# A hybrid attention step: the reciprocal ahead of a shared tile's transposes, its second half parted a block later, and a one-operand select on GpSimd

## The chip, the cores and the metric

The kernel runs on one core of a Trainium2 chip. The metric is the time of one execution on the device in microseconds; the figure for the kernel before is the median of three runs. The engines are named as the profile names them: PE is TensorE, with PEld its weight loads; DVE is VectorE, ACT is ScalarE, POOL is GpSimd, SP is SyncE, which issues DMAs.

## The reference

One layer with two parallel mixers over 1024 latent tokens and 128 context tokens, width 1024, head size 64, 8 query heads and 2 key heads in each mixer. Mixer A attends to all keys. Mixer B attends to a band of 128 tokens on either side and to the context, with a learned sink logit in the softmax. The part that the change touches is mixer B:

```python
valid = (jnp.abs(rel)[None] <= WINDOW) & (abs_j >= 0) & (abs_j < n)
s_band = jnp.where(valid[None, :, None, None], s_band, NEG_INF)
...
s = jnp.concatenate([sink_column(sink, kv, s_ctx.shape[:-1]), s_ctx, s_band], axis=-1)
p = jax.nn.softmax(s, axis=-1).astype(v_lat.dtype)
p_ctx = p[..., 1:1 + n_ctx]
p_band = p[..., 1 + n_ctx:]
o = (jnp.einsum('bnkgqs,bskd->bnqkgd', p_ctx, v_ctx)
     + jnp.einsum('bnkgqs,bnskd->bnqkgd', p_band, vband))
```

Both outputs are multiplied with a SiLU gate, put side by side, multiplied with `w_out` and added to the residual.

## The kernel before

After the projections the attention runs over units `(t, m, g)`: token tile `t` of 128 queries, mixer `m` (0 is A, 1 is B), key head `g` with its four query heads. They stand in the order `(1,0,0), (1,1,0), (1,0,1), (1,1,1), (2,0,0)` and so on, so units with an odd number are of mixer B. A unit of mixer A has nine key blocks, one of mixer B four (three for the first and last tile), and each block is one step of the main loop. At a step `s` the loop runs what has been put off to it (`tick`, filled by `later`), makes the weights of the step's block (`scores`), runs what the list `due` holds for the step, issues some matmuls of the output projection, and multiplies the weights of the block of three steps ago with the values (`values`). Nothing is reordered afterwards: on each engine the instructions stand in the order in which the code issues them, and each engine works its own list in order.

Products are made of two parts, a rounded `ph` and the rest `pl`, so a block of weights is exponentiated on ScalarE (L1305), rounded there (L1309, or L1290 and L1298 in mixer B), and the rest is made on GpSimd (L1313, L1291) or VectorE (L1299). `values` multiplies both parts (L1323, L1326).

A unit of mixer B gets its weights ahead, while the unit of mixer A before it runs. `weight_items` makes the scores with queries on the partitions (L1057, L1058), VectorE adds the mask (L1061), and ScalarE exponentiates them into `pen` and sums the rows (L1047). `finish` puts off the rest: the sink's exponential (`sinks`, L1091), its addition to the sum on GpSimd (`total`, L1094), and two steps after the weights the merging of `pair`. `divide` takes the reciprocal of the sum on VectorE (L1097), at the first step of the unit. One step later `turned` transposes the reciprocals on TensorE (`pti`, L1110), `put` copies them (L1114) and sends them to memory, and later they come back in rows and scale the unit's gates (L1120, L1106).

In the twelve *paired* units (mixer B, `1 < t < 8`) the band's first and last block share one tile. The first block has weights only where key >= query, the last only where key <= query, and both have the diagonal. `pair` therefore copies the last block into the empty half of the first on VectorE (L1015) and keeps of the last block only the diagonal, by a product with the identity on GpSimd (L1016). One step before the unit starts, `unpair` transposes the shared tile, four heads in one bank of PSUM (`st_pair`, L1024), and parts it: one VectorE instruction writes the first block's weights (L1026), a second copies the last block's over the diagonal (L1027). Blocks 1 and 2 of the unit are transposed as they come (L1297).

The PSUM banks that matter: tag B has two, shared by `st` and `st_pair`; tag A has two, shared by `pmx` (score maxima of a later unit of mixer A, L985, reduced on VectorE by L986 and at last L994), `sn` and `pti`.

Of the kernel before, what the change touches and what calls it, by code (L numbers as in the profile page):

```python
# [9 lines left out]
F32 = mybir.dt.float32  # L10
F32R = mybir.dt.float32r
BF16 = mybir.dt.bfloat16
I16 = mybir.dt.int16
AF = mybir.ActivationFunctionType
ALU = mybir.AluOpType
# [4 lines left out]
P = 128  # L20
# [54 lines left out]
EX_AT = (2, 2, 5)  # L75
ROWS_AT = (1, 1, 4, 6)
# [41 lines left out]
def hybrid_step(ctx, tc, x_prompt, x_sample, cache_k_a, cache_v_a, cache_k_b, cache_v_b,  # L118
# [3 lines left out]
    nc = tc.nc  # L122
# [13 lines left out]
    def later(n, f):  # L136

        agenda.setdefault(now[0] + n, []).append(f)
# [13 lines left out]
    def bank(tag, name):  # L152
        return ps.tile([P, 512], F32, tag=tag, name=name, bufs=BANKS[tag])
# [11 lines left out]
    ident_r = cst.tile([P, P], F32R, name="ident_r")  # L165
# [165 lines left out]
    with tc.tile_pool(name="st", bufs=2, side="right") as st:  # L331
# [4 lines left out]
                                channel_multiplier=1)  # L336
# [214 lines left out]
        for j in range(1, KT + 3):  # L551
# [68 lines left out]
            if KT - 2 <= j < KT:  # L620
# [3 lines left out]
                c0, n = W_QA.cols[0]  # L624
# [50 lines left out]
    with tc.tile_pool(name="qt", bufs=2, side="right") as qt:  # L675
# [29 lines left out]
        def query(pq, m, t, tabs, n=1):  # L705
# [19 lines left out]
            def rotated():  # L725

                qf = qt.tile([P, 4, 2, HD], F32, tag="qf", name=f"qf{nm}", bufs=3)
                out = qf.rearrange("p h g d -> p g h d")
                pair = lambda a: a.rearrange("p (g h) d -> p g h d", g=2)
                if t:  # L730
                    nc.vector.tensor_tensor(out, *(pair(a) for a in v["rot"]), op=ALU.add)
                else:
                    nc.vector.tensor_tensor(
                        out, pair(v["qn"]), gain4[:, 2 * m, :].unsqueeze(1).unsqueeze(1).to_broadcast([P, 2, 4, HD]),
                        op=ALU.mult)
                v["qf"] = qf
# [24 lines left out]
        for m in range(2):  # L761
            w, nxt = ((W_QA, W_QB), (W_QB, W_KV))[m]
            ts = list(range(1, NT)) + [0]
            for t in ts:
# [3 lines left out]
                if (m, t) in ((0, ts[-2]), (1, ts[GATE_AT[0]])):  # L768
                    n = len(wg) // 2
# [88 lines left out]
    def window(t):  # L858

        return (0 if t == 1 else POS[t - 2]), (12 if t == NL else POS[t] + 1)  # L860
# [6 lines left out]
    with ktp:  # L867
# [62 lines left out]
        for n, t in enumerate(KV_ORDER):  # L930
            if n < AHEAD:
                tick()
                pk, v = pks[n]
# [21 lines left out]
    qtile, qbtile, mxtile, sgl = {}, {}, {}, {}  # L955
    penat = {}
# [11 lines left out]
    def max_items(i):  # L968
# [37 lines left out]
                out.append(lambda h=h, b=b: item(h, b))  # L1006
        return out, finish

    def paired(t):

        return 1 < t < NL

    def pair(i):
        prev, nxt = (penat[i][:, :, o : o + P] for o in (0, 3 * P))
        nc.vector.copy_predicated(prev, mask[:, 0:P].bitcast(I16).unsqueeze(1).to_broadcast([P, 4, P]), nxt)  # L1015
        nc.gpsimd.tensor_tensor(nxt, nxt, ident_r.bitcast(F32).unsqueeze(1).to_broadcast([P, 4, P]), op=ALU.mult)  # L1016

    def unpair(i):

        prev, nxt = (penat[i][:, :, o : o + P] for o in (0, 3 * P))  # L1020
        over = mask[:, 3 * P : 4 * P].unsqueeze(1).to_broadcast([P, 4, P])
        s = bank("B", f"st{i}_pair")
        for h in range(4):
            nc.tensor.transpose(s[:, P * h : P * h + P], prev[:, h], ident_r.bitcast(F32))  # L1024
        s4 = s.rearrange("p (h n) -> p h n", h=4)
        nc.vector.scalar_tensor_tensor(prev, over, 0.0, s4, op0=ALU.is_ge, op1=ALU.mult)  # L1026
        nc.vector.copy_predicated(nxt, mask[:, 3 * P : 4 * P].bitcast(I16).unsqueeze(1).to_broadcast([P, 4, P]), s4)  # L1027

    def weight_items(i):

        t, m, g = units[i]
        v = {}

        def small(name):
            return qs.tile([P, 4], F32, tag=name, name=f"{name}{i}")

        def first(n):
            if t:
                penat[i] = qp2[0].tile([P, 4, 512], F32, tag="pen", name=f"pen{i}")[:, :, 0:n]
            else:  # L1040
                penat[i] = w3.tile([P, 512], F32, tag="pe", name=f"pen{i}", bufs=PES).rearrange(
                    "p (h n) -> p h n", h=4)
            for x in ("nm", "sum", "ex", "inv"):
                v[x] = small(x)

        def exp(h, s, scale):
            nc.scalar.activation(penat[i][:, h], s, AF.Exp, bias=v["nm"][:, h : h + 1], scale=scale,  # L1047
                                 accum_out=v["sum"][:, h : h + 1])

        def item(h):  # L1050
            p0, p1_ = window(t)
            n = P * (p1_ - p0)
            if h == 0:
                first(n)
            lhs = qtile[i][:, P * h : P * h + P]
            s = bank("DEEE"[h] if i == 3 else "A", f"sn{i}_{h}")[:, 0:n]
            nc.tensor.matmul(s, lhs, khb[:, g, p0:p1_, :], start=True, stop=False)  # L1057
            nc.tensor.matmul(s, lhs, klb[:, g, p0:p1_, :], start=False, stop=True)  # L1058
            m0 = P if t == 1 else 0

            nc.vector.tensor_tensor_reduce(s, s, mask[:, m0 : m0 + n], -1.0, nsink[:, 4 * g + h : 4 * g + h + 1],  # L1061
                                           op0=ALU.add, op1=ALU.min, accum_out=v["nm"][:, h : h + 1])
            later(1, lambda: exp(h, s, -1.0))

        def prompt():
            first(P)
            s = bank("A", f"sn{i}")
            for h in range(4):
                hs = slice(P * h, P * h + P)
                nc.tensor.matmul(s[:, hs], qtile[i][:, hs], khp[:, 2 + g, :], start=True, stop=False)  # L1070
                nc.tensor.matmul(s[:, hs], qtile[i][:, hs], klp[:, 2 + g, :], start=False, stop=True)
            mx = small("mx4")
            nc.vector.tensor_reduce(mx, s.rearrange("p (h n) -> p h n", h=4), axis=AX.X, op=ALU.max)
            nc.vector.scalar_tensor_tensor(v["nm"], mx, -1.0, nsink[:, 4 * g : 4 * g + 4], op0=ALU.mult, op1=ALU.min)
            for h in range(4):
                exp(h, s[:, P * h : P * h + P], 1.0)

        def finish():
            nc.gpsimd.tensor_tensor(v["ex"], v["nm"], sink[:, 4 * g : 4 * g + 4], op=ALU.add)
            if paired(t):  # L1080
                later(PAIR_AT, lambda: pair(i))
            if t:
                for n, f in zip(EX_AT if i > 3 else EX_EARLY, (sinks, total, divide)):
                    later(n, f)
            else:
                sinks()
                later(1, total)
                later(1, divide)

        def sinks():  # L1090
            nc.scalar.activation(v["ex"], v["ex"], AF.Exp)  # L1091

        def total():
            nc.gpsimd.tensor_tensor(v["sum"], v["sum"], v["ex"], op=ALU.add)  # L1094

        def divide():
            nc.vector.reciprocal(v["inv"], v["sum"])  # L1097
            if t == 0:
                for h in range(4):
                    nc.vector.tensor_scalar(penat[i][:, h], penat[i][:, h], v["inv"][:, h : h + 1], None, op0=ALU.mult)  # L1100
                return

            later(ROWS_AT[0], turned)
            later(ROWS_AT[1], put)
            later(ROWS_AT[2], rows)
            later(ROWS_AT[3], lambda: nc.gpsimd.tensor_tensor(sgl[i], sgl[i], v["rows"], op=ALU.mult))  # L1106

        def turned():
            v["pt"] = bank("A", f"pti{i}")[0:4, 0:P]
            nc.tensor.transpose(v["pt"], v["inv"], ident_r.bitcast(F32))  # L1110

        def put():
            iv = spare[0:4, 512 : 512 + P]
            (nc.vector.tensor_copy if i < 2 else nc.scalar.copy)(iv, v["pt"])  # L1114
            nc.sync.dma_start(r_dram[i // 2], iv)

        def rows():
            v["rows"] = spare[:, 512:768].rearrange("p (c n) -> p c n", c=2)
            for s in range(2):
                nc.sync.dma_start(v["rows"][HD * s : HD * s + HD],  # L1120
                                  r_dram[i // 2].rearrange("(c s) n -> s c n", s=2)[s : s + 1].to_broadcast([HD, 2, P]))

        return ([lambda h=h: item(h) for h in range(4)] if t else [prompt]), finish
# [42 lines left out]
    mask = qp.tile([P, 512], BF16, name="mask", bufs=1)  # L1166
# [116 lines left out]
    def scores(i, b, blk):  # L1283
# [3 lines left out]
        if m == 1 and paired(t) and blk[0] in (0, 3):  # L1287
            p = penat[i][:, :, P * blk[0] : P * blk[0] + P]
            ph4, pl4 = (a.rearrange("p (h n) -> p h n", h=4) for a in (ph, pl))
            nc.scalar.copy(ph4, p)  # L1290
            nc.gpsimd.tensor_tensor(pl4, p, ph4, op=ALU.subtract)  # L1291
            return ph, pl
# [138 lines left out]
    slots, start = [], []  # L1431
# [8 lines left out]
    def put(s, f):  # L1440
        due.setdefault(s, []).append(f)
# [23 lines left out]
    for i, (t, m, g) in enumerate(units):  # L1465
        if m and paired(t):
            put(start[i] - 1, lambda i=i: unpair(i))

    for k, at in enumerate(HELD):
        put(at, lambda k=k: held_gates(k))  # L1470
# [92 lines left out]
```

## Time and profile before

| | before |
|---|---|
| median of 3 runs | 703.16 us (703.07 to 703.47) |
| the profiled execution | 703.9 us, its span 702.2 us |
| granted TensorE clock | 0.999 |
| COPY_PREDICATED L1015 (12 times) | 754 ns |
| SCALAR_TENSOR_TENSOR L1026 (12 times) | 677 ns |
| COPY_PREDICATED L1027 (12 times) | 732 ns |
| RECIPROCAL L1097 (18 times, 12 of them paired) | 160 ns |
| transposes of the shared tile L1024 | 48 of 272 ns |

The durations are medians. The span runs from the first instruction to the last; some 1.7 us of the execution lie around it. A row of the timeline gives the start, the time from the start to the end, the engine, the line, the operation, output and inputs, and how many such rows follow each other; in brackets stands the idle time ahead and what ended it. A matmul's row begins when it is issued and ends when its last result is modelled to be out, so rows of following matmuls overlap.

### The profile page before, as it was taken

Reading aid. Unit: us, or ns where it says so; the run is one execution under the profiler, and the core shown is the slowest. Engines: PE = TensorE matmul, PEld = TensorE weight load, DVE = VectorE, ACT = ScalarE, POOL = GpSimd, SP = SyncE. Lnnn points to the kernel's source line nnn. Section 1 sums busy time; section 2 is a strip of 40 time slices with the busy share of each in tenths; the row PEclk is TensorE's granted clock in tenths of the full one; section 3 lists DMA queues with packets and bytes.
Section 4 is the critical chain, followed back from the end, with each engine's and each line's share of the span. In section 5 each row is a group of like instructions: output and inputs, shape, how many; then the busy total and the mean of one; then the engine's idle time right before and its main releaser. Section 6 shows DMA issues by size and latency. Waiting matters only on the chain.

```text
span 702.2 us, 10666 instructions
## 1 busy us (share of the span) xinstructions
PE 688.8 (98%) x3493; PEld 554.3 (79%) x3493; DVE 470.7 (67%) x1025; ACT 408.5 (58%) x848; POOL 387.4 (55%) x392
## 2 busy tenths in 40 slices
PE   8999999999999999999999999999999999999997
PEld 4679988878788889987777777787777777877876
DVE  4775258968778845756867677676776676675563
ACT  5666312412423433198876887787778768877770
POOL 3556033232223421278787867777786778686751
PEclk9999999999999999999999999999999999999999
DMA  8961283358443116423122121212221221212323
GB/s 342 405 244 61 79 304 76 90 151 262 113 115 112 34 42 218 129 92 102 46 83 76 45 84 53 90 40 75 67 84 32 83 75 45 84 54 90 96 78 120
DMA packets 54231, 78.50 MB, mean 112 GB/s; under 512 B 6952, under 2 KB 25496, under 8 KB 54176
## 3 DMA queue, kind: packets, MB, share of 16 engines
q1 hardware_dynamic: 45936, 65.86, 28.3%
q10 hardware_dynamic: 8240, 11.96, 6.3%
q8 instruction: 27, 0.44, 0.3%
q14 instruction: 28, 0.23, 0.1%
HBM read 58.63 MB, written 19.18 MB: 111 GB/s over the span
## 4 chain that ended last, share of the span: by engine, by line
PE 88%; DVE 6%; POOL 2%; issue 1%; ACT 1%; DMA 1%; SPq 0%; POOLq 0%; ACTq 0%; DVEq 0%
PE po L1404 13%; PE pv L1326 6%; PE pv L1323 5%; PE pq L268 5%; PE pq L266 5%; PE pq L267 5%; PE st L1303 4%; PE st L1302 4%; PE pmx L985 4%; PE pv L1325 4%; PE pg L280 3%; PE pg L276 3%; PE pg L281 3%; PE pk L267 2%; PE pk L268 2%; PE pk L266 2%
## 5 line engine op out<-in xcount | busy, mean ns | idle before, releaser
L1313 POOL TENSOR_TENSOR pl<-pe,ph 128x512 fp32r<-128x512 f32 x130 | 167.3, 1296 | 62.3 <-ACT ph L1309 49.2
L986 DVE TENSOR_REDUCE mx<-pmx 128x1 f32<-128x384 f32 x192 | 100.6, 550 | 50.1 <-PE pmx L985 49.6
L1305 ACT ACTIVATE pe<-st 128x512 f32<-128x512 f32 x146 | 86.7, 594 | 23.8 <-PE st L1303 22.7
L1309 ACT CAST ph<-pe 128x512 fp32r<-128x512 f32 x146 | 90.6, 621 | 5.5
L1323 PE MATMUL pv<-ph,v_hi 128*128 128x512 f32 x208 | 83.4, 401 | 0.1
L1326 PE MATMUL pv<-pl,v_hi 128*128 128x512 f32 x208 | 82.2, 395 | 0.9 <-POOL pl L1313 0.7
L184 POOL TENSOR_TENSOR rs_q<-ms_q,mhalf 128x8 f32<-128x8 f32 x18 | 34.1, 1897 | 80.8 <-DVE ms_q L182 80.8
L1061 DVE CUSTOM_DVE_ANT_0 sn<-sn,mask,nsink 128x512 f32<-128x512 f32 (+1 forms) x64 | 46.3, 724 | 43.8 <-PE sn L1058 41.4
L1404 PE MATMUL po<-wo,ogh 128*128 128x512 f32 (+1 forms) x224 | 73.3, 388 | 0.0
L985 PE MATMUL pmx<-kha,qt 128*128 128x384 f32 x192 | 59.7, 357 | 0.2 <-DVE mx L986 0.2
L1325 PE MATMUL pv<-ph,v_lo 128*64 128x512 f32 x146 | 57.7, 395 | 0.0
L1303 PE MATMUL st<-qb,kla 68*128 68x512 f32 x144 | 57.3, 398 | 0.0
L1302 PE MATMUL st<-qt,kha 128*128 128x512 f32 x144 | 57.1, 397 | 0.0
L1326 PEld LDWEIGHTS pv<-pl,v_hi 128*128 128x128 f32 x208 | 39.0, 188 | 18.4 <-POOL pl L1313 1.2
L1047 ACT ACTIVATE pen<-sn,nm 128x512 f32<-128x512 f32 (+2 forms) x72 | 44.9, 625 | 6.6 <-DVE nm L1061 3.1
L1404 PEld LDWEIGHTS po<-wo,ogh 128*128 128x128 f32 x224 | 41.0, 188 | 6.4 <-ACT ogh L1366 0.3
L1323 PEld LDWEIGHTS pv<-ph,v_hi 128*128 128x128 f32 x208 | 39.2, 188 | 8.1 <-issue 0.6
L1291 POOL TENSOR_TENSOR pl<-pen,ph 128x512 fp32r<-128x512 f32 x24 | 30.8, 1285 | 26.0 <-PE pv L1323 26.0
L744 ACT CAST qo0q<-ptq 128x512 fp32r<-128x512 f32 x18 | 10.6, 586 | 57.3 <-PE ptq L741 53.1
L1404 PE MATMUL po<-wo,ogl 128*128 128x512 f32 (+1 forms) x112 | 43.6, 389 | 0.0
L985 PEld LDWEIGHTS pmx<-kha,qt 128*128 128x128 f32 x192 | 35.3, 190 | 9.4 <-DVE mx L986 1.2
L466 POOL TENSOR_TENSOR h<-hf,h 128x256 fp32r<-128x256 f32 (+2 forms) x32 | 27.3, 876 | 19.8 <-ACT h L460 10.0
(260 smaller groups left out, 1768.7 us busy)
## 6 DMA issues: line engine op xcount, KB each, us to landing
qt<-qd SPq DMA_DIRECT2D x36, 256.0 KB, 2.9
wm<-in_w_mod_ss_dram SPq DMA_DIRECT2D x7, 1024.0 KB, 11.6
qd<-qo0q ACTq DMA_DIRECT2D x36, 128.0 KB, 2.4
qd<-qo1q ACTq DMA_DIRECT2D x36, 128.0 KB, 2.4
sgl<-gd SPq DMA_DIRECT2D x35, 128.0 KB, 2.5
out_dram<-yt SPq DMA_DIRECT2D x17, 256.0 KB, 2.1
xn<-in_x_sample_dram SPq DMA_DIRECT2D x8, 512.0 KB, 7.0
wg<-in_w_mod_g_dram SPq DMA_DIRECT2D x4, 1024.0 KB, 8.6
```

Source lines behind the costliest of these rows:

```text
L266: nc.tensor.matmul(out, h_at(0, i, k, tok), w.hi[k], start=(k == 0), stop=False)
L985: nc.tensor.matmul(pm[:, 0:384], lhs, kha[:, g, 3 * b : 3 * b + 3, :], start=True, stop=True)
L986: nc.vector.tensor_reduce(mx[:, h, b : b + 1], pm[:, 0:384], axis=AX.X, op=ALU.max)
L1302: nc.tensor.matmul(s, kh, qtile[i], start=True, stop=False)
L1303: nc.tensor.matmul(s, kl, qbtile[i], start=False, stop=True)
L1305: nc.scalar.activation(pe, s, AF.Exp)
L1309: nc.scalar.copy(ph, pe)
L1313: nc.gpsimd.tensor_tensor(pl, pe, ph, op=ALU.subtract)
L1323: nc.tensor.matmul(pv, two, ph, start=(b == 0), stop=False)
L1325: nc.tensor.matmul(pv[0:64, :], vl, ph, start=False, stop=False)
L1326: nc.tensor.matmul(pv, two, pl, start=False, stop=last)
L1404: nc.tensor.matmul(po[n, q.start], a, wo_parts[KT * n + k][lo][:, q], start=(k == KS[0] and p == 0), stop=(k == KS[-1] and p == 2))
```

## The change

For the paired units `divide` is no longer put off to the unit's first step: it is kept in `divided` and called at the head of `unpair`, in the step before, ahead of the transposes of the shared tile. What follows `divide` is put off by one step more, so it keeps its step. The second half of the parting, the COPY_PREDICATED, becomes `unpair_rest` and runs one step later. On GpSimd the product with the identity becomes an `affine_select`, which reads only the tile and writes zero off the diagonal. `sinks` and `total` keep their steps, and units that are not paired are as before.

```diff
+    divided = {}
...
     def pair(i):
         prev, nxt = (penat[i][:, :, o : o + P] for o in (0, 3 * P))
         nc.vector.copy_predicated(prev, mask[:, 0:P].bitcast(I16).unsqueeze(1).to_broadcast([P, 4, P]), nxt)
-        nc.gpsimd.tensor_tensor(nxt, nxt, ident_r.bitcast(F32).unsqueeze(1).to_broadcast([P, 4, P]), op=ALU.mult)
+        nc.gpsimd.affine_select(out=nxt, in_=nxt, pattern=[[0, 4], [-1, P]], compare_op=ALU.is_equal, fill=0.0, base=0,
+                                channel_multiplier=1)
+
+    shared = {}
 
     def unpair(i):
 
-        prev, nxt = (penat[i][:, :, o : o + P] for o in (0, 3 * P))
+        divided.pop(i)()
+        prev = penat[i][:, :, 0:P]
         over = mask[:, 3 * P : 4 * P].unsqueeze(1).to_broadcast([P, 4, P])
         s = bank("B", f"st{i}_pair")
         for h in range(4):
             nc.tensor.transpose(s[:, P * h : P * h + P], prev[:, h], ident_r.bitcast(F32))
-        s4 = s.rearrange("p (h n) -> p h n", h=4)
-        nc.vector.scalar_tensor_tensor(prev, over, 0.0, s4, op0=ALU.is_ge, op1=ALU.mult)
-        nc.vector.copy_predicated(nxt, mask[:, 3 * P : 4 * P].bitcast(I16).unsqueeze(1).to_broadcast([P, 4, P]), s4)
+        shared[i] = s.rearrange("p (h n) -> p h n", h=4)
+        nc.vector.scalar_tensor_tensor(prev, over, 0.0, shared[i], op0=ALU.is_ge, op1=ALU.mult)
+
+    def unpair_rest(i):
+        over = mask[:, 3 * P : 4 * P].bitcast(I16).unsqueeze(1).to_broadcast([P, 4, P])
+        nc.vector.copy_predicated(penat[i][:, :, 3 * P : 4 * P], over, shared.pop(i))
...
-            if t:
+            if paired(t):
+                later(EX_AT[0], sinks)
+                later(EX_AT[1], total)
+                divided[i] = divide
+            elif t:
                 for n, f in zip(EX_AT if i > 3 else EX_EARLY, (sinks, total, divide)):
                     later(n, f)
...
-            later(ROWS_AT[0], turned)
-            later(ROWS_AT[1], put)
-            later(ROWS_AT[2], rows)
-            later(ROWS_AT[3], lambda: nc.gpsimd.tensor_tensor(sgl[i], sgl[i], v["rows"], op=ALU.mult))
+            o = int(paired(t))
+            later(ROWS_AT[0] + o, turned)
+            later(ROWS_AT[1] + o, put)
+            later(ROWS_AT[2] + o, rows)
+            later(ROWS_AT[3] + o, lambda: nc.gpsimd.tensor_tensor(sgl[i], sgl[i], v["rows"], op=ALU.mult))
...
         if m and paired(t):
             put(start[i] - 1, lambda i=i: unpair(i))
+            put(start[i], lambda i=i: unpair_rest(i))
```

How the instructions move is shown at unit 11 (token tile 3, second key head), whose neighbours of mixer A are units 10, 12 and 14. The number behind a tile's name is its unit; line numbers of the changed kernel differ by the lines added. First VectorE, where the unit's shared tile is parted; before:

```order
L986 TENSOR_REDUCE mx12_4674<-pmx12_3_1_4943 128x1
L986 TENSOR_REDUCE mx12_4674<-pmx12_3_2_4946 128x1
L1026 SCALAR_TENSOR_TENSOR pen11_4757<-mask_2970,st11_pair_4951 128x4x128
L1027 COPY_PREDICATED pen11_4757<-mask_2970,st11_pair_4951 128x4x128
L1097 RECIPROCAL inv11_4761<-sum11_4759 128x4
L986 TENSOR_REDUCE mx14_4967<-pmx14_0_0_4968 128x1
L994 TENSOR_REDUCE m_nat0_109<-mx12_4674 128x4
L986 TENSOR_REDUCE mx14_4967<-pmx14_0_1_4989 128x1
```

And the same place of VectorE in the changed kernel:

```order
L986 TENSOR_REDUCE mx12_4673<-pmx12_3_1_4943 128x1
L986 TENSOR_REDUCE mx12_4673<-pmx12_3_2_4946 128x1
L1110 RECIPROCAL inv11_4761<-sum11_4759 128x4
L1032 SCALAR_TENSOR_TENSOR pen11_4757<-mask_2970,st11_pair_4952 128x4x128
L986 TENSOR_REDUCE mx14_4966<-pmx14_0_0_4967 128x1
L1036 COPY_PREDICATED pen11_4757<-mask_2970,st11_pair_4952 128x4x128
L994 TENSOR_REDUCE m_nat0_109<-mx12_4673 128x4
L986 TENSOR_REDUCE mx14_4966<-pmx14_0_1_4989 128x1
```

The reciprocal has moved up past the two instructions that part the tile, and the COPY_PREDICATED down past one reduction; the rows around them are the same.

On GpSimd the rows around the select of unit 11 are these in the changed kernel (`sum11` is the reciprocal's input, `pl10` the rest of the weights of unit 10, whose product is running):

```order
L1327 TENSOR_TENSOR pl10_5_4865<-pe10_5_4869,ph10_5_4864 128x512
L1368 TENSOR_TENSOR spare_3486<-spare_3486,sgl9_4639 128x256
L1018 AFFINE_SELECT pen11_4757<-pen11_4757 128x4x128
L1107 TENSOR_TENSOR sum11_4759<-sum11_4759,ex11_4760 128x4
L1327 TENSOR_TENSOR pl10_6_4893<-pe10_6_4897,ph10_6_4892 128x512
L1327 TENSOR_TENSOR pl10_7_4907<-pe10_7_4911,ph10_7_4906 128x512
L1327 TENSOR_TENSOR pl10_8_4935<-pe10_8_4939,ph10_8_4934 128x512
```

Before, the third row was a TENSOR_TENSOR of `pen11` and `ident_r` (L1016); no row has moved.

On TensorE, which waits for both, these rows stand around the transpose of the reciprocals in the changed kernel:

```order
L1030 MATMUL st11_pair_4952<-ident_r_99,pen11_4757 128x128 x4
L1337 MATMUL pv10_4833<-ph10_5_4864,v_hi_2396 128x512
L1339 MATMUL pv10_4833<-ph10_5_4864,v_lo_2397 64x512
L1340 MATMUL pv10_4833<-pl10_5_4865,v_hi_2396 128x512
L985 MATMUL pmx14_0_0_4967<-kha_2390,qt14_4855 128x384
L1337 MATMUL pv10_4833<-ph10_6_4892,v_hi_2396 128x512
L1339 MATMUL pv10_4833<-ph10_6_4892,v_lo_2397 64x512
L1340 MATMUL pv10_4833<-pl10_6_4893,v_hi_2396 128x512
L1124 MATMUL pti11_4974<-ident_r_99,inv11_4761 4x128
L1311 MATMUL st11_1_4980<-ident_r_99,pen11_4757 128x128 x4
L985 MATMUL pmx14_0_1_4989<-kha_2390,qt14_4855 128x384
```

Nothing has moved there: TensorE, ScalarE and SyncE have the same rows in the same order in both kernels.

## The prediction

> **What bounds the kernel now.** I read the page's busy line and its chain of waits first, to see which engine carries the end of the program.
>
> ```profile
> PE 688.8 (98%) x3493; PEld 554.3 (79%) x3493; DVE 470.7 (67%) x1025; ACT 408.5 (58%) x848; POOL 387.4 (55%) x392
> ...
> PE 88%; DVE 6%; POOL 2%; issue 1%; ACT 1%; DMA 1%; SPq 0%; POOLq 0%; ACTq 0%; DVEq 0%
> ```
>
> TensorE is busy for 98% of the span and holds 88% of the chain. So the change can save no more than what TensorE loses in waits around it, and it costs something only where it makes TensorE wait. The twelve places that the change touches lie between 350 and 622 us, so I next took the busy times of that stretch, and then TensorE's waits in it, longest first (what waited, for whom, us in total, times, longest).
>
> ```profile
> 340.00:625.00 285.00, 279.85 (x1308) 220.81 (x1307) 199.87 (x419) 218.82 (x439) 218.90 (x216) 1.00 0.22 68
> ```
>
> ```profile
> PE pti L1110 <- DVE inv L1097: 4.2, 11, 0.5
> PE pv L1326 <- POOL pl L1313: 0.7, 1, 0.7
> PE pmx L985 <- DVE mx L986: 0.2, 1, 0.2
> ```
>
> The stretch lasts 285.00 us and TensorE is busy for 279.85, which leaves 5.15 us idle. The three rows add up to 5.1, so nothing else is hidden there. Most of it, 4.2 us in eleven waits, is one thing: the small transpose `pti` (L1110) waits for the reciprocal `inv` of VectorE (L1097). Only twelve units are paired, and in the twelfth another wait covers this one (below). The idle figure is too low, however. The timeline of unit 11, one of the twelve, shows why:
>
> ```profile
> 424.68 1.01 DVE L986 TENSOR_REDUCE mx<-pmx 128x1 f32<-128x384 f32 x2
> 425.50 0.34 PE L985 MATMUL pmx<-kha,qt 128*128 128x384 f32 x1
> 425.61 0.68 DVE L1026 SCALAR_TENSOR_TENSOR pen<-mask,st_pair 128x512 f32<-128x512 bf16 x1
> 425.68 0.40 PE L1323 MATMUL pv<-ph,v_hi 128*128 128x512 f32 x1
> 425.92 0.40 PE L1325 MATMUL pv<-ph,v_lo 128*64 128x512 f32 x1
> 426.15 0.40 PE L1326 MATMUL pv<-pl,v_hi 128*128 128x512 f32 x1
> 426.20 0.73 DVE L1027 COPY_PREDICATED pen<-mask,st_pair 128x512 f32<-128x512 int16 x1
> 426.37 0.62 ACT L1290 CAST ph<-pen 128x512 fp32r<-128x512 f32 x1 [0.92 <-PE pv L1325]
> 426.82 0.16 DVE L1097 RECIPROCAL inv<-sum 128x4 f32<-128x4 f32 x1
> 426.91 0.52 DVE L986 TENSOR_REDUCE mx<-pmx 128x1 f32<-128x384 f32 x1
> 427.04 0.27 PE L1110 MATMUL pti<-ident_r,inv 128*4 128x128 f32 x1 [0.49 <-DVE inv L1097]
> 427.35 0.15 DVE L994 TENSOR_REDUCE m_nat<-mx 128x4 fp32r<-128x12 f32 x1
> 427.66 0.45 PE L985 MATMUL pmx<-kha,qt 128*128 128x384 f32 x1
> 428.23 1.29 POOL L1291 TENSOR_TENSOR pl<-pen,ph 128x512 fp32r<-128x512 f32 x1
> 428.63 0.60 PE L1297 MATMUL st<-ident_r,pen 128*128 128x128 f32 x4
> ```
>
> The matmuls before `pti` start 0.23 us apart (425.68, 425.92, 426.15) while each row is 0.40 long, since they overlap. After the last one the next could start at 426.38. `pti` starts at 427.04, so TensorE loses 0.66 us, not the 0.49 that shows as idle. In the units of the other key head it loses less:
>
> ```profile
> 402.11 0.40 PE L1326 MATMUL pv<-pl,v_hi 128*128 128x512 f32 x1
> 402.75 0.27 PE L1110 MATMUL pti<-ident_r,inv 128*4 128x128 f32 x1 [0.25 <-DVE inv L1097]
> ```
>
> Here it is 402.75 - 402.11 - 0.23 = 0.41. Each idle entry thus hides 0.40 - 0.23 = 0.17 us, and the eleven waits are worth 4.2 + 11 x 0.17 = **6.1 us**.
>
> The Trainium skill ("Perfetto Trace Analysis", Identifying the Most-Contended Engine) says that matmul busy time is no good measure of the distance to the limit because matmuls are pipelined. By the busy time the eleven waits would give 4.2; by the starts in these rows, which bear that sentence out, they give 6.1.
>
> **The reciprocal, part by part.** Why does `pti` wait? VectorE works in order, and in unit 11 it is continuously busy from 424.68: two reductions, the SCALAR_TENSOR_TENSOR L1026 (425.61), the COPY_PREDICATED L1027 (426.20), and only then the reciprocal (426.82 to 426.98). Its own input has long been there, as GpSimd's rows show:
>
> ```profile
> 422.42 1.29 POOL L1016 TENSOR_TENSOR pen<-pen,ident_r 128x512 f32<-128x512 f32 x1
> 423.68 0.19 POOL L1094 TENSOR_TENSOR sum<-sum,ex 128x4 f32<-128x4 f32 x1
> 423.83 3.76 POOL L1313 TENSOR_TENSOR pl<-pe,ph 128x512 fp32r<-128x512 f32 x3
> ```
>
> The sum (L1094) is done at 423.68 + 0.19 = 423.87, and VectorE is free of the two reductions at 424.68 + 1.01 = 425.69. Afterwards the reciprocal stands right behind these reductions. I take the steps between starts from the same rows: reciprocal to next 0.09 (426.82 to 426.91), L1026 to next 0.59, a reduction to next 0.44 (426.91 to 427.35). The reciprocal starts at 425.61 and ends by 425.77. That is 0.6 ahead of 426.38, when TensorE wants it, and in the units of the other head as well (reciprocal 1.2 us earlier, want 0.41 earlier). So the whole wait goes: 6.1 us.
>
> What is late next? L1026 starts at 425.70 instead of 425.61, and behind it is ScalarE's cast L1290, which moves from 426.37 to about 426.46 and ends at 427.08. Its reader, GpSimd's L1291, starts at 428.23 because GpSimd is still on other work. So these 0.09 us cost nothing. If that cover were gone, they would cost 12 x 0.09 = 1.1 us. The reduction of `pmx14_0_0` moves forward from 426.91 to 426.29 and ends at 426.81. It frees the bank of the matmul that stands at 427.66, whose turn is now 427.00, 0.66 earlier. After the 0.06 that TensorE took to follow the reciprocal (426.98 to 427.04) that leaves 0.13 us. The COPY_PREDICATED starts at 426.29 + 0.44 = 426.73 instead of 426.20 and ends at 427.46. Two things wait for it: the cast of the second half, three blocks later, and the transposes of block 2 (428.63, then 427.97), which take the bank it reads. That leaves 0.5 us. The five rows of VectorE have the same total in either order, so the reduction L994 still ends at about 427.50, and everything behind it starts as before or sooner. The orders of TensorE, ScalarE and the DMA queue are row for word the same, so no DMA is moved: the copy of `pti`, its DMA and the loads behind it keep their places in the program.
>
> **The select on GpSimd.** L1016 becomes AFFINE_SELECT, which the trace shows once, on a quarter of the columns:
>
> ```profile
> L1016 POOL TENSOR_TENSOR pen<-pen,ident_r 128x512 f32<-128x512 f32 x12 | 15.5, 1294 | 0.0
> L335 POOL TENSOR_SCALAR_AFFINE_SELECT ident<-ident 128x128 f32<-128x128 f32 x1 | 0.3, 292 | 0.1
> L334 POOL MEMSET ident<- 128x128 f32 x1 | 0.2, 204 | 0.3 <-POOLq L1547 0.3
> L362 POOL MEMSET sil<- 128x256 f32 x1 | 0.3, 311 | 0.0
> L1369 POOL TENSOR_TENSOR ogl<-spare,ogh 128x256 fp32r<-128x256 f32 x34 | 25.0, 736 | 0.0
> L369 POOL CAST ident_r<-ident 128x128 fp32r<-128x128 f32 x1 | 0.7, 747 | 0.0
> ```
>
> The two-operand product takes 1.29 us twelve times. The one AFFINE_SELECT takes 0.292 for 128 columns. For 512 columns I add 384 columns by the step between the MEMSETs of 128 and 256 columns (311 - 204 over 128, or 0.84 ns each): 0.292 + 0.32 = 0.61 us. The upper near bound is four times the small one, 1.17; that agrees with the two-operand step from L1369 to L1016, (1294 - 736) / 256 = 2.2 ns each, which gives 1.13. The far bound is the slowest one-operand row here, CAST L369 with 747 ns for 128 columns: 2.99. The low bound is 0.45, the small select plus half of my step. I take **0.61**, as that is built on the only row of the operation itself, so GpSimd gains 0.68 us in each paired unit.
>
> Where does that reach TensorE? In eleven units nowhere: GpSimd finishes the first `pl` behind the sum at 423.83 + 3.76 / 3 = 425.08, and TensorE takes it at 426.15, with 1.07 to spare. Only in unit 5, the first paired one, is TensorE waiting for GpSimd:
>
> ```profile
> 350.69 1.27 POOL L1016 TENSOR_TENSOR pen<-pen,ident_r 128x512 f32<-128x512 f32 x1
> 351.92 0.20 POOL L1094 TENSOR_TENSOR sum<-sum,ex 128x4 f32<-128x4 f32 x1
> 352.76 3.76 POOL L1313 TENSOR_TENSOR pl<-pe,ph 128x512 fp32r<-128x512 f32 x3
> 352.96 0.40 PE L1325 MATMUL pv<-ph,v_lo 128*64 128x512 f32 x1
> 354.10 0.50 PE L1326 MATMUL pv<-pl,v_hi 128*128 128x512 f32 x1 [0.74 <-POOL pl L1313]
> ```
>
> L1326 could start at 352.96 + 0.23 = 353.19 and starts at 354.10: 0.91 lost, because the `pl` in progress since 352.76 ends at about 354.0. Its chain runs back through the sum to the select without a gap, so a select shorter by 0.68 brings 0.68 of the 0.91. The reciprocal of this unit is not late: the sum ends at 351.92 + 0.20 = 352.12, and `pti` has its turn only behind the L1326 of 354.10, after 353.6 even when that starts 0.68 sooner.
>
> The sum is 6.1 + 0.68 = **6.8 us**. The profiled execution took 703.9 us with a span of 702.2, and becomes 697.1. The median of the runs shown is 703.16, 0.74 below it, so the prediction is 703.16 - 6.8 = **696.4**. With the near bounds of the select (0.45 to 1.17) the first unit brings 0.12 to 0.84. With 0.3 either way for the steps and the spread between runs this case spans 695.9 to 697.3.
>
> **The rivals.** *A part comes back as the next wait.* The thinnest margin is the 0.13 us of the bank that `pmx14_0_0` holds. If VectorE's rows up to that reduction run 0.5 longer than I reckon, for instance because the L1026 behind the reciprocal starts late, TensorE loses 0.37 in each of eleven units, or 4.1, and the gain is 2.7: 700.5. For it speaks the small margin; against it, all these durations are read off the same rows.
>
> *All of it is given back later.* If TensorE runs ahead, the engines that feed it may not follow. In the stretch ScalarE and GpSimd are busy for 218.8 and 218.9 of 285 us, or 77%. At a pace 2% higher that becomes 79%. If a loop through them sets the pace, the time stays at 703.2. Against it: outside these waits TensorE has one wait of 0.7 and one of 0.2 in the whole stretch.
>
> *Slower, through a slow select.* If AFFINE_SELECT over 512 columns is later than the product by D, the sum and the three `pl` behind it are late by D. In the eleven units TensorE then loses D - 1.07 at L1326, ahead of `pti`, and in the first one D + 0.91: together 12 D - 10.9, against 6.1 + 0.9 = 7.0 lost now. It turns from gain to loss at D = 1.49, a select of 2.8 us. At the rate of the CAST, 2.99 us, D is 1.70 and the loss 9.5: 2.5 us slower, 705.7. Against it: at the rate of the CAST the small select would have taken 747 ns, and it took 292. The Trainium skill ("GPSIMD Engine Reference", section 3.1) gives about 12 cycles per element for data-dependent branching on this engine. By that rule, at its 1.2 GHz, the select would be an estimated 5.1 us, D 3.8 and the time 731; but the small select would then have taken 1.28 us, so the trace speaks against the rule applying to this operation.
>
> *The change doesn't do what it says*: the reciprocal now waits for the sum and holds VectorE up. The sum is there 1.8 us ahead in unit 11, and only a select over 3.1 us would make it late, so this belongs to the slow select.
>
> **How the numbers follow.** The forecast has 0.78, the part that comes back 0.10, all given back 0.05, the slow select 0.07. The likeliest case gives 696.4. The range begins at 695.5, with all of unit 5's wait and 0.2 us of spread more, and reaches into the second case, to 699.2, so that less than 2 in 10 is left out. A measurement of this kernel can tell about 0.2%, 1.4 us, from no change: faster 0.88, same 0.05, slower 0.07.
>
> **What would show it.** In the profile after, the row of `pti` waiting for `inv` should be gone from TensorE's waits, with `pti` starting 0.23 after the matmul ahead of it. The idle time of the stretch should fall from 5.15 to under 1 us. The select's row should read about 610 ns, and the wait of `pv` for `pl` should shrink to about a third. A new row of TensorE waiting for `mx` or for `pen` would be the first rival, a new row waiting for `pl` twelve times the third.

## The result and the profile after

| | before | after |
|---|---|---|
| median | 703.12 us (703.07 to 703.47, 4 runs) | 694.72 us (694.65 to 694.84, 4 runs) |
| the profiled execution | 703.9 us, span 702.2 us | 694.65 us, span 692.9 us |

The changed kernel takes 0.988 of the time of the kernel before (95% interval 0.9863 to 0.9897), 8.4 us less. Forecast were 6.8 us less and a range down to 695.5. The way was right, and the result lies 0.8 us below the range. The two spans differ by 9.3 us. That is 0.9 more than the medians, because the profiled execution before reached the first product of the query projection (L266) at 81.18 us and the one after at 80.29, in code that is the same. So differences of places are taken below, or medians, and not spans.

On the page of the changed kernel stand these two lines, the busy engines and the chain that ended last:

```profile
PE 686.3 (99%) x3493; PEld 555.2 (80%) x3493; DVE 470.6 (68%) x1025; ACT 407.2 (59%) x848; POOL 379.9 (55%) x392
...
PE 96%; ACT 1%; DMA 1%; DVE 1%; POOL 0%; issue 0%; SPq 0%; ACTq 0%; POOLq 0%; DVEq 0%
```

TensorE holds 96% of the chain now, against 88%. The stretch with the paired units, by busy time of each engine, and TensorE's waits in it, which are one row:

```profile
340.00:615.00 275.00, 274.68 (x1301) 220.19 (x1300) 198.35 (x416) 216.02 (x436) 210.84 (x215) 1.00 0.22 70
```

```profile
PE pmx L985 <- DVE mx L986: 0.2, 1, 0.2
```

Idle are 275.00 - 274.68 = 0.32 us, where there were 5.15. The waits for the reciprocal and for GpSimd's `pl` are gone from this view. Rows of unit 11 in the timeline, with others left out, show how:

```profile
421.57 1.01 DVE L986 TENSOR_REDUCE mx<-pmx 128x1 f32<-128x384 f32 x2
422.50 0.17 DVE L1110 RECIPROCAL inv<-sum 128x4 f32<-128x4 f32 x1
422.58 0.66 DVE L1032 SCALAR_TENSOR_TENSOR pen<-mask,st_pair 128x512 f32<-128x512 bf16 x1
423.05 0.40 PE L1340 MATMUL pv<-pl,v_hi 128*128 128x512 f32 x1
423.15 0.55 DVE L986 TENSOR_REDUCE mx<-pmx 128x1 f32<-128x384 f32 x1
423.28 0.27 PE L1124 MATMUL pti<-ident_r,inv 128*4 128x128 f32 x1
423.39 0.60 PE L1311 MATMUL st<-ident_r,pen 128*128 128x128 f32 x4
423.62 0.74 DVE L1036 COPY_PREDICATED pen<-mask,st_pair 128x512 f32<-128x512 int16 x1
423.76 0.44 PE L985 MATMUL pmx<-kha,qt 128*128 128x384 f32 x1
423.85 0.25 ACT L1128 COPY spare<-pti 4x128 f32<-4x128 f32 x1
424.25 0.15 DVE L994 TENSOR_REDUCE m_nat<-mx 128x4 fp32r<-128x12 f32 x1
424.74 0.60 PE L1311 MATMUL st<-ident_r,pen 128*128 128x128 f32 x4
```

The reciprocal starts at 422.50, right behind the two reductions, and is done 0.6 us before `pti` (L1124) comes up. `pti` starts 0.23 after the product ahead of it (423.05 to 423.28), so nothing is lost. The first half of the parting (422.58), the reduction of `pmx14_0_0` (423.15), the second half (423.62) and the reduction L994 (424.25) stand in the order and at the distances of the forecast. The select is this group:

```profile
L1018 POOL TENSOR_SCALAR_AFFINE_SELECT pen<-pen 128x512 f32<-128x512 f32 x12 | 7.6, 631 | 0.0
```

It takes 631 ns; forecast were 610. In the first paired unit, unit 5, TensorE still waits for GpSimd, but less:

```profile
352.03 0.40 PE L1339 MATMUL pv<-ph,v_lo 128*64 128x512 f32 x1
352.55 0.49 PE L1340 MATMUL pv<-pl,v_hi 128*128 128x512 f32 x1
```

L1340 could start at 352.03 + 0.23 = 352.26 and starts at 352.55. So 0.29 us are lost where 0.91 were.

All of that is as predicted, and it adds up to 6.0 for the reciprocal and 0.6 for unit 5. Matching TensorE's products one by one between the two traces, the eleven `pti` gain 5.97 us and unit 5's wait 0.61. But there is a third place that gains, the score product `pmx` (L985) behind the first four transposes that follow `pti`. It gains 0.11 to 0.15 us in each of the twelve units, some 1.7 us in all. That is what the prediction lacks, so I looked at this place in the trace of before, again in unit 11:

```profile
427.15 0.60 PE L1297 MATMUL st<-ident_r,pen 128*128 128x128 f32 x4
427.35 0.25 ACT L1114 COPY spare<-pti 4x128 f32<-4x128 f32 x1 [0.36 <-PE pti L1110]
427.65 0.19 PEld L985 LDWEIGHTS pmx<-kha,qt 128*128 128x128 f32 x1
428.98 0.59 PE L985 MATMUL pmx<-kha,qt 128*128 128x384 f32 x2
```

Behind the four transposes of block 1 the product starts 427.66 - 427.15 = 0.51 us after the first of them. Behind those of block 2 (428.63 in the prediction's rows) it is 428.98 - 428.63 = 0.35. Something costs 0.15 at the first place. Its weight load starts 0.05 us after ScalarE's copy of the transposed reciprocals (L1114, 427.35 + 0.25 = 427.60). In the changed kernel the copy is at 423.85 and the product already at 423.76, so it no longer waits for it.

The order of the instructions doesn't explain this, since the product has the same place in it; the banks do. `pmx` and `pti` share two banks of PSUM, and the pool decides as the program is built which tile takes which. In the built programs, unit 11:

```
             before  changed
pmx14_0_0      2       3
pti11          3       2
pmx14_0_1      3       3
pmx14_0_2      2       2
```

Before, the second score product `pmx14_0_1` took the bank of `pti11` and so had to wait until ScalarE had read it. In the changed kernel it takes the bank of `pmx14_0_0`, which VectorE's reduction has freed, and `pti`'s bank goes to the third product.

### The profile page after: what moved, and what is told of

Its sections match the earlier page's. It is cut to its first block, busy times and chain, and to the rows that moved or that the text cites. A ratio compares the mean times of both kernels' runs of the same rounds, so it can differ in the third digit from the quotient of the medians.

```text
span 692.9 us, 10678 instructions
## 1 busy us (share of the span) xinstructions
PE 686.3 (99%) x3493; PEld 555.2 (80%) x3493; DVE 470.6 (68%) x1025; ACT 407.2 (59%) x848; POOL 379.9 (55%) x392
## 4 chain that ended last, share of the span: by engine, by line
PE 96%; ACT 1%; DMA 1%; DVE 1%; POOL 0%; issue 0%; SPq 0%; ACTq 0%; POOLq 0%; DVEq 0%
PE po L1418 14%; PE pv L1340 7%; PE pv L1337 7%; PE pmx L985 5%; PE st L1316 5%; PE st L1317 5%; PE pv L1339 5%; PE pq L268 5%; PE pq L266 5%; PE pq L267 5%; PE pg L280 3%; PE pg L276 3%; PE pg L281 3%; PE pk L267 2%; PE pk L268 2%; PE pk L266 2%
## 5 line engine op out<-in xcount | busy, mean ns | idle before, releaser
L1340 PE MATMUL pv<-pl,v_hi 128*128 128x512 f32 x208 | 82.2, 395 | 0.3 <-DVE pl L1313 0.2
L985 PE MATMUL pmx<-kha,qt 128*128 128x384 f32 x192 | 59.6, 357 | 0.2 <-DVE mx L986 0.2
L1340 PEld LDWEIGHTS pv<-pl,v_hi 128*128 128x128 f32 x208 | 39.1, 188 | 17.8 <-POOL pl L1327 0.6
L985 PEld LDWEIGHTS pmx<-kha,qt 128*128 128x128 f32 x192 | 35.3, 190 | 7.7 <-DVE mx L986 1.2
```

The costliest lines, as they stand in the source:

```text
L985: nc.tensor.matmul(pm[:, 0:384], lhs, kha[:, g, 3 * b : 3 * b + 3, :], start=True, stop=True)
L1340: nc.tensor.matmul(pv, two, pl, start=False, stop=last)
```

## The experiments

The theory after the result: of the 8.4 us, 6.0 are the wait for the reciprocal, 1.7 to 1.8 the bank, 0.6 the select in unit 5. The rivals: the late product has to do with TensorE's stall and not with the bank; and the reciprocal's new place carries the gain, as the prediction had it, or some other of the three edits does. Times are medians beside runs of the kernel before on the same chip:

| kernel | us | before beside it | difference | ratio, 95% interval |
|---|---|---|---|---|
| e1, before, banks of the changed kernel | 701.14 | 703.07 | -1.93 | 0.9972 (0.9961 to 0.9982) |
| e2, changed, banks of before | 698.25 | 703.07 | -4.82 | 0.9931 (0.9918 to 0.9943) |
| e3, reciprocal's move alone | 698.77 | 703.07 | -4.30 | 0.9939 (0.9927 to 0.9952) |
| e4, later parting alone | 695.40 | 703.07 | -7.67 | 0.9892 (0.9877 to 0.9907) |
| e5, select alone | 703.42 | 703.85 | -0.43 | 0.9992 (0.9983 to 1.0001) |
| e6, changed, without the select | 696.31 | 703.85 | -7.54 | 0.9891 (0.9878 to 0.9905) |
| e7, changed, unit 5's select later | 695.55 | 703.85 | -8.30 | 0.9881 (0.9867 to 0.9894) |
| e8, parting and select | 694.79 | 703.12 | -8.33 | 0.9881 (0.9865 to 0.9898) |
| e9, changed kernel again | 694.69 | 703.12 | -8.43 | 0.9879 (0.9864 to 0.9894) |

On the chip of e5 to e7 all kernels, the one before too, spread over about 1 us or more, so there the differences are less sure than on the others.

**e1 and e2: the banks exchanged.** The tiles of tag A get their bank from a list, taken from the other kernel's build; nothing else changes. The list itself is left out here.

```diff
...
     def bank(tag, name):
+        if tag == "A":
+            k = A_BANKS[len(a_used)]
+            a_used.append(name)
+            return ps.tile([P, 512], F32, tag="A" + k, name=name, bufs=1)
         return ps.tile([P, 512], F32, tag=tag, name=name, bufs=BANKS[tag])
```

Expected of the kernel before with the changed kernel's banks:

> The kernel before with one thing changed: the score products take the two banks of tag A in strict turn (the bank list of the changed kernel), so that in each paired unit the second score product behind the transpose of the reciprocals no longer takes that transpose's bank. Theory (the gain that the prediction lacks is the wait for ScalarE's copy of the transposed reciprocals, 0.147 us in twelve units): 1.7 us less than before, 701.4, while the wait of the transpose for the reciprocal stays at about 4.2 us of idle time in eleven places. Rival (that product starts late because the weight loads have lost their lead after TensorE's stall, whatever the bank): same as before, 703.1.

It takes 1.93 us less. The two longest waits of TensorE itself in the stretch (what waited, for whom, us, times, longest):

```profile
PE pti L1121 <- DVE inv L1108: 4.2, 11, 0.5
PE pv L1337 <- POOL pl L1324: 0.8, 1, 0.8
```

The wait for the reciprocal stands there unchanged, 4.2 us of idle in eleven places. So the stall is as before, and yet the product behind it is no longer late. In unit 11 (L1308 are the transposes, L1125 is ScalarE's copy, L996 the score product):

```profile
425.74 0.60 PE L1308 MATMUL st<-ident_r,pen 128*128 128x128 f32 x4
425.94 0.25 ACT L1125 COPY spare<-pti 4x128 f32<-4x128 f32 x1 [0.36 <-PE pti L1121]
426.09 0.43 PE L996 MATMUL pmx<-kha,qt 128*128 128x384 f32 x1
```

The product starts 426.09 - 425.74 = 0.35 behind the first transpose, while the copy still runs until 426.19. In the trace it gains 0.15 in each of the twelve units. The rival falls; the late product was the bank.

Expected of the changed kernel with the banks of before:

> The changed kernel with the bank list of the kernel before: the second score product takes the bank of the transposed reciprocals again. Theory (the bank decides): ScalarE copies the reciprocals only behind its cast of the first block, which ends about 0.6 us after TensorE has reached the transpose, so TensorE waits about 0.5 us in the six units of the second key head and 0.23 in the others: 4.2 us more than the changed kernel, 698.9, with a row of TensorE's weight load waiting for ScalarE twelve times. Rival (weight loads after the stall): no stall is left, so the same as the changed kernel, 694.7.

It takes 698.25, 3.5 us more than the changed kernel. Unit 11 in its timeline (L1135 is `pti`, L1139 ScalarE's copy of it, L1315 the cast ahead of the copy, L996 the score product):

```profile
424.11 0.27 PE L1135 MATMUL pti<-ident_r,inv 128*4 128x128 f32 x1
424.17 0.62 ACT L1315 CAST ph<-pen 128x512 fp32r<-128x512 f32 x1 [0.98 <-DVE pen L1043]
424.21 0.60 PE L1322 MATMUL st<-ident_r,pen 128*128 128x128 f32 x4
424.70 0.25 ACT L1139 COPY spare<-pti 4x128 f32<-4x128 f32 x1
425.00 0.44 PE L996 MATMUL pmx<-kha,qt 128*128 128x384 f32 x1 [0.19 <-ACT spare L1139]
```

ScalarE casts the first block until 424.79, copies the reciprocals by 424.95, and the product starts 0.05 later. It would have had its turn 0.35 after the first transpose (424.21), at 424.56, so 0.4 us are lost. In the units of the first key head it is 0.15, not the 0.23 that I expected, and in the others 0.42 to 0.44, not 0.5; together they are the miss, 3.5 against 4.2. The banks are forced in the same way in e1 and e2, and one gains where the other loses, so it is the list that counts and not the forcing.

**e3: the reciprocal's move alone.** This is the changed kernel with both halves of the parting together again and with the product for the select.

```diff
...
-            put(start[i] - 1, lambda i=i: unpair(i))
-            put(start[i], lambda i=i: unpair_rest(i))
+            put(start[i] - 1, lambda i=i: (unpair(i), unpair_rest(i)))
```

> The kernel before with the reciprocal alone moved ahead of the transposes; both instructions that part the tile stay together, the product with the identity stays, and the banks come out as in the kernel before. Theory: the wait for the reciprocal goes (6.0), but the wait for the bank of the transposed reciprocals grows from 0.15 to 0.23 to 0.5 us in each unit: 6.0 + 1.8 - 4.3 = 3.5 us less than before, 699.6. Rival (the prediction: the reciprocal's place carries nearly all of the gain): 6.1 less, 697.0.

It gains 4.30, between the two, nearer to 3.5. Product by product the `pti` gain 5.97 us, as the prediction had it, and the score products behind them lose 1.59, because this kernel has the banks of before. In e2, where these banks are forced, they lose 1.61. Its waits of TensorE and of its weight loads:

```profile
PEld pmx L985 <- ACT spare L1127: 2.5, 6, 0.4
PE pmx L985 <- ACT spare L1127: 1.1, 6, 0.2
PE pv L1339 <- POOL pl L1326: 0.8, 1, 0.8
```

The product waits for ScalarE's copy in the six units of the second key head: 2.5 us for the weight loads. Counted from the transposes of the shared tile in unit 11, `pti` comes 0.67 earlier than before (2.00 against 2.67), but the copy, which stands behind ScalarE's cast of the first block, only 0.39 (2.59 against 2.98).

**e4: the later parting alone.** The reciprocal stays at the unit's first step.

```diff
-        nc.vector.copy_predicated(nxt, mask[:, 3 * P : 4 * P].bitcast(I16).unsqueeze(1).to_broadcast([P, 4, P]), s4)
+        shared[i] = s4
...
             put(start[i] - 1, lambda i=i: unpair(i))
+            put(start[i], lambda i=i: unpair_rest(i))
```

> The kernel before with the second half of the parting alone moved a block later; the reciprocal stays at the unit's first step, where it now stands right behind the first half of the parting, the product with the identity stays, and the banks come out as in the changed kernel. Theory: the reciprocal ends 0.3 us before TensorE wants it in the units of the first key head and about 0.05 after it in the others, so 5.7 of the 6.0 go and the bank's 1.7 with them: 7.4 us less than before, 695.7. Rival (the reciprocal's move is needed): the wait for it stays near 0.4 to 0.66 us in each unit and only the bank's 1.7 goes: 701.4.

It gains 7.67 of the 8.4. Unit 11 in its timeline (L1103 is the reciprocal, L1116 `pti`):

```profile
423.21 0.67 DVE L1026 SCALAR_TENSOR_TENSOR pen<-mask,st_pair 128x512 f32<-128x512 bf16 x1
423.74 0.40 PE L1332 MATMUL pv<-pl,v_hi 128*128 128x512 f32 x1
423.81 0.17 DVE L1103 RECIPROCAL inv<-sum 128x4 f32<-128x4 f32 x1
423.90 0.52 DVE L986 TENSOR_REDUCE mx<-pmx 128x1 f32<-128x384 f32 x1
424.03 0.27 PE L1116 MATMUL pti<-ident_r,inv 128*4 128x128 f32 x1
424.34 0.73 DVE L1033 COPY_PREDICATED pen<-mask,st_pair 128x512 f32<-128x512 int16 x1
```

With the COPY_PREDICATED out of the way (424.34) the reciprocal comes at 423.81, one row later than in the changed kernel, and is done at 423.98. `pti` follows at 424.03, where its turn was 423.74 + 0.23 = 423.97. It loses 0.06 us in this unit, 0.05 to 0.06 in each of the six of the second key head, and nothing in the others. And this kernel has the banks of the changed one: the built programs with the later parting (e4, e6, e7, e8 and the changed kernel) all have the new list, those without it (before, e3, e5) the old one.

**e5 and e6: the select.** Expected of the select alone:

> The kernel before with the one-operand select alone. Theory: GpSimd gains 0.66 us in each of the twelve paired units, and it reaches TensorE in the first of them alone, where the wait for the rest of the weights shrinks from 0.9 to 0.25: 0.65 us less than before, 702.4. Rival (GpSimd's lead helps TensorE in the other units too, or the two engines disturb each other less): more than 1.5 us less, under 701.6.

It gains 0.43, with an interval that takes in no change, so the time alone doesn't settle it. The waits do: those for the reciprocal are untouched, and unit 5's weight load waits 0.6 us for `pl` where it waits 1.2 with the product (e6, below). Product by product TensorE gains 0.59 in unit 5 and nothing in the others.

```profile
PE pti L1111 <- DVE inv L1098: 4.2, 11, 0.5
PEld pv L1327 <- POOL pl L1314: 0.6, 1, 0.6
```

Expected of the changed kernel with the product in the select's place:

> The changed kernel with the product with the identity in place of the select. Theory: 0.6 us more than the changed kernel, 695.3, all of it in the first paired unit, where TensorE waits 0.9 us for GpSimd again. Rival (the select also carries part of the gain in the other eleven units): 696 or more.

It gains 7.54, so against the 8.4, measured on another chip, the select is worth 0.86 by the medians, with this chip's spread in it. Product by product it loses 0.63 us in one place, unit 5, where the wait is back:

```profile
PEld pv L1339 <- POOL pl L1326: 1.2, 1, 1.2
PE pv L1339 <- POOL pl L1326: 0.8, 1, 0.8
```

**e7: unit 5's select a block later.**

```diff
...
+        if i == 5:
+            later(1, select)
+        else:
+            select()
```

> The changed kernel, in the first paired unit alone with the select one block later, so that on GpSimd it stands behind the rest of the weights for which TensorE is still waiting there. Theory: that wait of 0.29 us and the 0.11 behind it go: 0.4 us less than the changed kernel, 694.3. Rival (the COPY_PREDICATED on VectorE, which writes over what the select left, now waits for it and holds up VectorE): no less than the changed kernel, 694.7 or more.

It gains 8.30 where the changed kernel gains 8.4 on other chips: nothing measurable. In unit 5 the first wait is gone (L1346 is the product that waited, L1019 the select):

```profile
351.75 0.64 POOL L1019 TENSOR_SCALAR_AFFINE_SELECT pen<-pen 128x512 f32<-128x512 f32 x1
351.90 0.39 PE L1345 MATMUL pv<-ph,v_lo 128*64 128x512 f32 x1
352.13 0.40 PE L1346 MATMUL pv<-pl,v_hi 128*128 128x512 f32 x1
352.36 2.53 POOL L1333 TENSOR_TENSOR pl<-pe,ph 128x512 fp32r<-128x512 f32 x2
352.42 0.75 DVE L1042 COPY_PREDICATED pen<-mask,st_pair 128x512 f32<-128x512 int16 x1
353.71 0.50 PE L1346 MATMUL pv<-pl,v_hi 128*128 128x512 f32 x1
```

The product starts at 352.13, in turn (351.90 + 0.23). But the select now stands ahead of the next two `pl`, the first of which ends only at about 353.65, and the next product waits for it until 353.71, 0.15 after its turn. The COPY_PREDICATED, which the rival blamed, started at 352.42, 0.03 after the select's end and 0.54 after the start of the reduction ahead of it (351.88), against 0.47 in the changed kernel. So the select held it up by 0.07 at the most, and no wait of TensorE's in the trace goes back to it. Neither theory had the mechanism: the wait moved by one product.

**e8 and e9: is the reciprocal's move needed at all?** e8 is e4 with the select; e9 is the changed kernel beside it.

> The kernel before with the parting a block later and the select, the reciprocal left at the unit's first step. Theory (once the second half of the parting is out of the way the reciprocal's place is worth nothing): the same as the changed kernel run beside it, within 0.2 us, about 8.3 us less than before. Rival (the reciprocal's move still carries a part): 0.7 us or more above the changed kernel.

> The changed kernel itself, run beside the kernel with parting and select alone: about 8.4 us less than before, in every theory.

694.79 and 694.69, with runs from 694.67 to 695.02 and 694.65 to 694.75: the same to 0.1 us. What e8 still pays for its reciprocal is small:

```profile
PEld pti L1117 <- DVE inv L1104: 2.0, 6, 0.3
PEld pv L1333 <- POOL pl L1320: 0.6, 1, 0.6
```

The weight loads wait 2.0 us in six units, but TensorE has other products in flight then, and its loss there is 0.05 to 0.06 in each. No kernel of these beats the changed one by more than the runs differ.

## Why the prediction was right, and where it was wrong

The way and both terms of the sum were right. The step that failed is a term that the sum put at nothing without a reason: the wait for the bank of the score product behind `pti`, 1.7 us in all. The prediction gave that product the wrong bank, and took the banks to be the same in both kernels.

- *The wait for the reciprocal goes, 6.1 us*: right. It was 5.97, read from the starts of products and not from the idle time of 4.2.
- *The select takes 0.61 us and reaches TensorE in unit 5 alone, for 0.68 us*: right. It takes 0.631 and brings 0.61; e5 and e6 show it in no other unit.
- *The reduction of `pmx14_0_0` "frees the bank of the matmul that stands at 427.66"*: this step was wrong. In the kernel before that matmul sat in the bank of `pti` and waited for ScalarE's copy, 0.15 us in each of twelve units. This loss was there to be gained and is missing from the sum: 1.93 us in e1, 1.7 in the changed kernel. 6.0 + 1.7 + 0.6 = 8.3, against 8.4 measured. That it was gained is luck, as no edit aimed at it. With the banks of before (e2) the changed kernel gains 4.82 and not 6.8: once the stall is gone, the wait for the copy grows, in six units from 0.15 to some 0.43. So the 6.8 that the prediction reckoned with unchanged banks was too much for those banks and too little for the ones that came.
- *"The three rows add up to 5.1, so nothing else is hidden there"*: this is why it was missed. The row of the four transposes ahead of the product is 0.60 long, but the product could start 0.35 after its start, so the row covers 0.25 us and a wait of 0.15 leaves no idle time. The prediction corrected eleven waits for such an overlap, 0.17 each, and did not look for others that it hides altogether. Rows of one kind at two places, 0.51 against 0.35, would have shown it.
- *"The orders of TensorE, ScalarE and the DMA queue are row for word the same"*: true, and not enough. The same rows stood in other banks, and what each waits for had changed.
- *The reciprocal's place carries the gain*: the prediction gave the 6.1 us to its move. e4 and e8 show that the later parting alone does it: with one 0.73 us instruction less ahead of it the reciprocal is in time, but for 0.06 in six units. e3 shows that its move alone gives 4.3, because the bank stays where it was and takes 1.6 back. The two edits reach the same wait, so their gains do not add.
- *The first rival, 0.13 us of margin at the bank of `pmx14_0_0`*: the margin was about zero. In unit 11 the reduction ends at 423.15 + 0.55 = 423.70 and the product starts at 423.76, 0.02 after its turn (423.39 + 0.35); in the other units of the second key head it loses up to 0.04. That is some 0.16 us in all, where the rival had 4.1.
- *The other rivals* did not come: nothing was given back, as the stretch has 0.32 us of idle time left, and the select was not slow, with 0.631 us.
- *The range* began at 695.5, with unit 5's whole wait gained. Its own parts give 703.16 - 6.1 - 0.91 - 0.3 - 0.2 = 695.65, not 695.5, and either way it had no room for a wait that the sum did not know.

Why the pool takes another bank when the parting is later was not tried. The kernels only show that it goes with the parting and not with the other two edits.

## What to carry to other kernels

Where matmuls overlap, measure a wait from start to start, and compare the same two instructions at several places: a wait shorter than the overlap (0.15 against 0.25 us here) shows in no idle time. A change that leaves an engine's order alone can still change which buffer each tile takes, and with it what each instruction waits for, so compare the buffers of the two builds too. Before you credit an edit with the end of a wait, ask whether another edit of the same change ends it alone.

## What the runs showed of the hardware that was not expected

GpSimd's one-operand select costs 0.292 us for 128 columns and 0.631 for 512, which on a straight line through the two is 0.88 ns per column and 0.18 us fixed. Its two-operand product needs 1.29 for the same 512. The 12 cycles per element that the Trainium skill ("GPSIMD Engine Reference", section 3.1) gives for data-dependent branching do not fit it: at the 1.2 GHz that the same page of the Trainium skill gives for the engine, they would be an estimated 5.1 us for 512 columns.
